# Down projections of a two-layer decoder trunk: second halves whose groups are added to the stream by DMAs, and a different set of 7-product k-tiles

## The chip, the cores and the metric

The kernel runs on one core of one Trainium2 chip. The metric is the device time of one execution in microseconds (us); lower is better. Three runs of the kernel before gave a median of 2252.42 us (2252.37 to 2252.44).

A core has TensorE (PE: matmuls, and PEld for its weight loads), VectorE (DVE), ScalarE (ACT), GpSimd (POOL) and SyncE (SP, which issues DMAs here). PE writes to PSUM banks, the other engines read and write SBUF and PSUM, and DMAs bring weights from HBM into SBUF.

## What is computed

The reference is a decoder trunk of two layers on a stream `h` of 256 tokens by 2048 features, in float32. The change lies in `conv_ffn`'s last product, `w_down`, of both layers.

```python
D_MODEL, SEQ, DEPTH, D_FF = 2048, 256, 2, 5632

def conv_ffn(xn, w_up, conv_w, conv_b, w_down):
    u = xn @ w_up
    # causal depthwise convolution of width 3 over the tokens -> c
    gate, val = jnp.split(c, 2, axis=-1)
    return (jax.nn.silu(gate) * val) @ w_down

def reference(x, ...):
    h = x
    for layer in range(DEPTH):
        if layer == 0:
            h = h + mlstm_mixer(rms_norm(h, a_norm[0]), ...)
        else:
            k_sh, v_sh = shared_kv(h, kv_norm, w_kv, positions)
            h = h + diff_attention(rms_norm(h, b_norm[0]), k_sh, v_sh, ...)
        h = h + conv_ffn(rms_norm(h, f_norm[layer]), w_up[layer], conv_w[layer],
                         conv_b[layer], w_down[layer])
    return rms_norm(h, final_norm)
```

## The kernel before

**Numbers and operands.** Every float32 operand is kept as a pair of float32r values, high and low part, and a product is made of three matmuls: high by high, low by high, high by low. The stream stays in SBUF as `stream`, 128 partitions by 2 token halves by 2048 features. Hidden features come in tiles of 128, called k-tiles.

**Weights.** They are read from HBM while the kernel runs. `granule` (from L360 on) loads 4 k-tiles by 512 columns (1 MB) into a tile `raw`, from a ring of 4 (RAW) that SP's queue fills; ACT casts the high part into a tile `w2` (L376) and DVE subtracts to make the low part (L377). `w2` has a ring of 5 tiles (HL): a cast waits until PE has used the tile that stood five before. One such pair of instructions prepares 2 k-tiles by 512 columns, or, in `gemm`, 4 k-tiles by 256.

**The down projection.** The 44 k-tiles of a layer are taken in two parts of 22, since the hidden tiles of one part fill the buffers; each part runs its up-projections (`gemm`) and then `gemm_sevenths` over four groups (NG) of 512 columns (G), and adds its result to the stream. A group accumulates both token halves in two PSUM banks (`acc`, called a and b in the code). At the k-tiles named in MIXED, four k-tiles (two at the end) are done by pairs with 7 products in place of 8, in the manner of Strassen: for two k-tiles and two token halves, 21 matmuls of width 256 stand for 12 of width 512. `sevenths` prepares their weights: DVE makes differences of weight blocks (L449 to L451), then for each pair ACT and DVE split the three plain blocks (768 elements a partition) and the four differences (1024), at L458 and L459. The sums of hidden tiles that they are multiplied with are made in the up-projection by `mix`. Parts of the products gather in two more banks (`mix`, called c and d).

**The end of a group.** `mixed_in` adds what lies in c and d to the stream: one copy by ACT (L572) and on DVE three adds of 256 (L573 to L575 and L576, with L573 and L574 making sums in the tile `mixed`) and two of 512 (L578, L579). `residual`'s `evac` then adds a and b (L587, 512 each). In layer 0's second part the attention's norm object takes the group over (`Norm.add`): ACT squares it (L224), PE transposes it a granule later (L231), and ACT and DVE make from the transposes the scaled pairs `x_at` (L306, L307) and a copy `kept` (L235). The last group of layer 1 is done apart (`finish`), the others by `evac_last`, which squares and multiplies with the last norm's gains.

**What sets the order.** The program is traced once. `tick` counts granules, and `later(n, fn)` traces a piece n granules on. The Tile scheduler then fixes each engine's instruction order by its own estimates and by what depends on what; an engine works its list strictly in this order, and semaphores hold it where an operand, a ring's tile or a bank isn't ready.

## Time and profile before

| | us |
|---|---|
| median of 3 runs | 2252.42 |
| the profiled execution | 2251.92 |
| its span, first to last instruction | 2250.0 |
| PE busy | 2238.2 |
| DVE busy | 1796.9 |
| ACT busy | 1297.7 |
| layer 0, second part: groups 0, 1, 2, 3 begin at | 1007.6, 1036.8, 1066.9, 1097.1 |
| attention's first product begins at | 1127.2 |

The times come from one profiled execution on the core. A row of groups gives the source line, engine, operation, output and inputs with their shapes, the count, and then busy time with the mean of one in ns, and the idle time just before with what released the engine. A row of the timeline gives start, length and the same names. The windows view gives the busy time of each engine in a stretch. The chain of waits is followed back from the last instruction to what released each step.

### The profile page before, as it was taken

Reading aid. Unit: us, or ns where it says so; the run is one execution under the profiler, and the core shown is the slowest. Engines: PE = TensorE matmul, PEld = TensorE weight load, DVE = VectorE, ACT = ScalarE, POOL = GpSimd, SP = SyncE. Lnnn points to the kernel's source line nnn. Section 1 sums busy time; section 2 is a strip of 40 time slices with the busy share of each in tenths; the row PEclk is TensorE's granted clock in tenths of the full one; section 3 lists DMA queues with packets and bytes.
Section 4 is the critical chain, followed back from the end, with each engine's and each line's share of the span. In section 5 each row is a group of like instructions: output and inputs, shape, how many; then the busy total and the mean of one; then the engine's idle time right before and its main releaser. Section 6 shows DMA issues by size and latency. Waiting matters only on the chain.

```text
span 2250.0 us, 33498 instructions
## 1 busy us (share of the span) xinstructions
PE 2238.2 (99%) x12859; PEld 1955.0 (87%) x12859; DVE 1796.9 (80%) x2980; ACT 1297.7 (58%) x2010; POOL 124.4 (6%) x305
## 2 busy tenths in 40 slices
...
GB/s 265 188 169 157 165 173 204 191 190 187 187 172 177 246 188 187 187 150 197 189 214 189 168 169 168 150 206 188 187 187 187 156 191 238 191 188 191 147 215 150
DMA packets 325348, 419.04 MB, mean 186 GB/s; under 512 B 9070, under 2 KB 238788, under 8 KB 325188
## 3 DMA queue, kind: packets, MB, share of 16 engines
...
q14 instruction: 59, 0.48, 0.1%
...
## 4 chain that ended last, share of the span: by engine, by line
PE 97%; DVE 1%; POOL 1%; issue 1%; ACT 0%; DMA 0%; DVEq 0%; SPq 0%; POOLq 0%
PE acc L411 54%; PE acc L503 16%; PE acc L437 12%; PE mix L493 6%; PE acc L493 4%; PE acc L634 2%; PE acc L521 1%; PE val_ps L335 1%; PE turn_ps L231 1%; POOL rs_u L279 0%; DVE w L377 0%; PE as_ps L972 0%; DMA pos_i<-in_positions_dram 0%; POOL rs_u L281 0%; PE gps L681 0%
## 5 line engine op out<-in xcount | busy, mean ns | idle before, releaser
L377 DVE TENSOR_TENSOR w<-raw,w 128x1024 fp32r<-128x1024 f32 x679 | 826.4, 1221 | 267.5 <-ACT w L376 265.6
L376 ACT ACTIVATE w<-raw 128x1024 fp32r<-128x1024 f32 x679 | 714.2, 1058 | 489.1 <-PE acc L411 322.4
L411 PE MATMUL acc<-x_f,w 128*128 128x512 f32 (+1 forms) x5632 | 987.8, 338 | 0.0
L411 PEld LDWEIGHTS acc<-x_f,w 128*128 128x128 f32 x5632 | 862.3, 188 | 122.3
L503 PE MATMUL acc<-w,hid 128*128 128x512 f32 x1080 | 268.2, 395 | 0.0
L503 PEld LDWEIGHTS acc<-w,hid 128*128 128x128 f32 x1080 | 195.5, 188 | 38.8
L411 PE MATMUL acc<-x_at,w 128*128 128x512 f32 (+1 forms) x1024 | 182.3, 338 | 0.0
L411 PEld LDWEIGHTS acc<-x_at,w 128*128 128x128 f32 x1024 | 156.8, 188 | 21.8 <-issue 0.3
L458 ACT ACTIVATE w<-diff 128x1024 fp32r<-128x1024 f32 x89 | 94.1, 1057 | 111.1 <-DVE diff L451 82.0
L417 ACT ACTIVATE low<-acc 128x256 f32<-128x256 f32 x216 | 78.8, 384 | 131.7 <-PE acc L411 128.8
L459 DVE TENSOR_TENSOR w<-diff,w 128x1024 fp32r<-128x1024 f32 x89 | 108.8, 1222 | 40.6 <-ACT w L458 39.9
L437 PE MATMUL acc<-w,x_a 128*128 128x512 f32 x576 | 138.1, 396 | 0.0
L437 PEld LDWEIGHTS acc<-w,x_a 128*128 128x128 f32 x576 | 107.0, 188 | 24.1
L493 PE MATMUL mix<-w,mix 128*128 128x256 f32 x801 | 119.5, 282 | 0.0
L418 DVE TENSOR_TENSOR acc<-acc,low 128x256 f32<-128x256 f32 x216 | 84.4, 430 | 38.6 <-ACT low L417 38.4
L493 PEld LDWEIGHTS mix<-w,mix 128*128 128x128 f32 x801 | 107.2, 188 | 2.4 <-DVE w L459 0.2
L848 ACT ACTIVATE c<-u,conv 128x256 f32<-128x256 f32 x176 | 98.2, 593 | 5.2 <-DVE u L846 4.8
L953 POOL TENSOR_TENSOR sw<-sw,sin_t 32x256 f32<-32x256 f32 x32 | 39.1, 1237 | 1043.2 <-DVE sw L952 992.7
L458 ACT ACTIVATE w<-raw 128x768 fp32r<-128x768 f32 x89 | 74.7, 839 | 37.5 <-PE acc L503 26.9
L437 PE MATMUL acc<-w,x_at 128*128 128x512 f32 x384 | 91.4, 396 | 0.0
L459 DVE TENSOR_TENSOR w<-raw,w 128x768 fp32r<-128x768 f32 x89 | 84.8, 952 | 3.0 <-ACT w L458 2.9
L493 PE MATMUL acc<-w,hid 128*128 128x256 f32 x450 | 86.4, 281 | 0.0
...
## 6 DMA issues: line engine op xcount, KB each, us to landing
...
```

The costliest lines, as they stand in the source:

```text
L376: act.activation(w2[:, :hc, 0], part, AF.Copy)
L377: dve.tensor_tensor(w2[:, :hc, 1], part, w2[:, :hc, 0].bitcast(F32), op=ALU.subtract)
L411: pe.matmul(to, a, b, start=(k == 0 and o == 0), stop=(k == kn - 1 and o == len(ops) - 1))
L417: act.activation(low, p[:, T:], AF.Copy)
L418: dve.tensor_tensor(p[:, :T], p[:, :T], low, op=ALU.add)
L437: pe.matmul(ps[t], a[:, s], b, start=(k == 0 and o == 0), stop=(k == kn - 1 and o == 2))
L458: act.activation(w2[:, :m, 0], src, AF.Copy)
L459: dve.tensor_tensor(w2[:, :m, 1], src, w2[:, :m, 0].bitcast(F32), op=ALU.subtract)
L493: pe.matmul(to, u, v, start=start and o == 0, stop=end and o == 2 and to is not a and to is not b, skip_group_check=True)
L503: pe.matmul(ps, u[:, s], v, start=(k0 + i == 0 and o == 0), stop=(k0 + i == kn - 1 and o == 2), skip_group_check=True)
L634: pe.matmul(ps[j], a, b, start=(k == 0 and o == 0 and j % 2 == 0), stop=(k == KD - 1 and o == 2), skip_group_check=True)
L848: act.activation(c, u, AF.Identity, bias=cw[:, 3, f:f + 1], scale=cw[:, 2, f:f + 1])
```

## The change

MIXED becomes two lists, one for each part. In the second part the 7-product k-tiles are now 2 to 5, 10 to 13 and 18 to 21: 12 where there were 10 (4 to 7, 12 to 15, 20 and 21). The plain k-tiles between them are 0 and 1, 6 to 9 and 14 to 17, and `granule` gets a slice of the weights for each of these stretches, so the first load of a group is half a load.

Groups 0 to 2 of layer 0's second part and groups 0 and 1 of layer 1's go through a new function `landed`. It copies part of c, and a and b, into SBUF tiles (ACT), makes the sums x and y of the mixed banks (four adds of 256 on DVE), and POOL issues four accumulating DMAs of 128 by 512 that add a, b, x and y to the stream in SBUF. What follows on the group (`Norm.add`, or `summed`, which holds the squares and gain products of `evac_last`) is traced nine granules later, and `behind` ties its squares on ACT and transposes on PE behind the last instruction traced so far on these engines. One more pair list per layer goes through `mix`. Group 3 of layer 0 and group 2 of layer 1 end as before.

```diff
@@ -38,7 +38,7 @@
 NG = D // G
 RAW = 4
 OUT_AT = (8, 10)
-MIXED = (4, 12, 20)
+MIXED = ((4, 12, 20), (2, 10, 18))
 HL = 5
 WARM, WARM_X = 28, 24
 X_AT = (0, 2, 3, 5, 6, 8, 9)
@@ -107,6 +107,17 @@
                 if i.name not in before and i.engine in last:
                     tc.add_manual_dep(i, last[i.engine], mybir.DependencyInfo(mybir.DependencyClass.NoSync, mybir.DependencyReason.DATA), reason="as_written")
                 last[i.engine] = i.name
+
+    @contextmanager
+    def behind():
+
+        traced = nc.cur_bb.bb.instructions
+        last = {i.engine: i.name for i in traced if i.engine in (act.engine, pe.engine)}
+        before = {i.name for i in traced}
+        yield
+        for i in traced:
+            if i.name not in before and i.engine in last:
+                tc.add_manual_dep(i, last[i.engine], mybir.DependencyInfo(mybir.DependencyClass.NoSync, mybir.DependencyReason.DATA), reason="behind")
 
 
     waiting, clock, loads = [], [0, 0], []
@@ -242,11 +253,17 @@
         def second(self, i):
             self.scaled(1, i, self.kept.pop(i))
 
-        def add(self, g):
-
-            self.squares(g)
+        def add(self, g, order=nullcontext):
+
+            with order():
+                self.squares(g)
+
+            def operands(i):
+                with order():
+                    self.operands(4 * g + 2 * i)
+
             for i in range(2):
-                later(1, lambda i=i: self.operands(4 * g + 2 * i))
+                later(1, lambda i=i: operands(i))
 
         def rstd(self, after=1):
 
@@ -495,7 +512,9 @@
                             tick()
                     k0 += 4
                 else:
-                    for i, (wh, wl) in enumerate(granule(w, col0 + g * G, G, k0, kn, raws, g)):
+                    since = max([0] + [k + 4 for k in at if k < k0])
+                    until = min([kn] + [k for k in at if k > k0])
+                    for i, (wh, wl) in enumerate(granule(w[since * P:until * P], col0 + g * G, G, k0 - since, until - since, raws, g)):
                         xh, xl, _ = xs[k0 + i]
                         for t, ps in enumerate((a, b)):
                             s = slice(t * P, (t + 1) * P)
@@ -578,8 +597,28 @@
         dve.tensor_tensor(both, both, u[1].rearrange("p (o n) -> p o n", o=1).broadcast_to([P, 2, T]), op=ALU.add)
         dve.tensor_tensor(stream[:, :, c0], d[:, :T].rearrange("p (o n) -> p o n", o=1).broadcast_to([P, 2, T]), stream[:, :, c0], op=ALU.add)
 
-    def residual(norm):
+    def landed(g, ps, mix, then):
+
+        (a, b), (c, d) = ps, mix
+        u = tmp("mx")
+        a2, b2, x, y = (block(F32, f"land_{n}") for n in "abxy")
+        act.activation(x[1], c[:, :T], AF.Copy)
+        dve.tensor_tensor(u, c[:, T:], x[1], op=ALU.add)
+        act.activation(a2[2], a, AF.Copy)
+        dve.tensor_tensor(y[1], d[:, T:], u, op=ALU.add)
+        act.activation(b2[2], b, AF.Copy)
+        dve.tensor_tensor(x[0], d[:, :T], u, op=ALU.add)
+        dve.tensor_tensor(y[0], d[:, :T], y[1], op=ALU.add)
+        for t, rows in ((0, a2), (1, b2), (0, x), (1, y)):
+            pool.dma_start(stream[:, t, g * G:(g + 1) * G], rows[2], accum_op=ALU.add)
+        later(9, then)
+
+    def residual(norm, by_dma=0):
+
         def evac(g, ps, mix=None):
+            if g < by_dma:
+                landed(g, ps, mix, lambda: norm.add(g, behind))
+                return
             if mix is not None:
                 mixed_in(g, mix)
             for t in range(2):
@@ -866,7 +905,7 @@
                     dve.tensor_tensor(c, c, conv_of[f], op=ALU.mult)
                     hidden[f] = split(c, f"hid{f}")
                     pair.append(c)
-                if 4 * (j // 2) in MIXED:
+                if any(k <= 2 * j < k + 4 for k in MIXED[part]):
                     mixed[2 * j] = mix(pair)
 
             for j in range(half // 2):
@@ -874,11 +913,11 @@
                 gemm(norm.sets[0], w_up[layer], D_FF + part * half * P, [j], evac_val)
             rows = w_down[layer, part * half * P:(part + 1) * half * P]
             if part == 0:
-                gemm_sevenths(hidden, mixed, rows, 0, range(NG), residual(None), MIXED)
+                gemm_sevenths(hidden, mixed, rows, 0, range(NG), residual(None), MIXED[part])
             elif finish is None:
-                gemm_sevenths(hidden, mixed, rows, 0, range(NG), evac_down, MIXED)
+                gemm_sevenths(hidden, mixed, rows, 0, range(NG), evac_down, MIXED[part])
             else:
-                gemm_sevenths(hidden, mixed, rows, 0, range(NG - 1), evac_down, MIXED)
+                gemm_sevenths(hidden, mixed, rows, 0, range(NG - 1), evac_down, MIXED[part])
                 finish(hidden, rows)
 
 
@@ -1058,7 +1097,7 @@
     gemm_sevenths(outs, outs_mixed, m_w_out[0], 0, [NG - 1], residual(norm_f0), OUT_AT[:1])
 
     norm_at = Norm([(gains, G_B), (gains, G_KV)], "at")
-    conv_ffn(0, norm_f0, residual(norm_at))
+    conv_ffn(0, norm_f0, residual(norm_at, 3))
     outs, outs_mixed = attention(norm_at)
     norm_f1 = Norm([(gains, G_F1)], "f1")
     gemm_tokens(outs, w_o[0], 0, range(2), residual(norm_f1), lead=2)
@@ -1074,24 +1113,32 @@
         return gain_rows[c0 // G][2][:, c0 % G:c0 % G + width]
 
     def evac_last(g, ps, mix=None):
-        if mix is not None:
-            mixed_in(g, mix)
         if g == 0:
 
             tc.keep_in_program_order(act.activation(work.tile([P, 1], F32, name="ahead", bufs=2), ones[:, 0:1], AF.Sqrt))
             for c in range(NG):
                 gain_rows.append(block(F32, f"gain_rows{c}"))
                 nc.sync.dma_start(gain_rows[c][2], final_norm[c * G:(c + 1) * G].rearrange("(o c) -> o c", o=1).broadcast_to([P, G]))
-        c0, width = g * G, G
-        if g == NG - 1:
-            width = T
+        if g < 2:
+            landed(g, ps, mix, lambda: summed(g, G, behind))
+            return
+        if mix is not None:
+            mixed_in(g, mix)
+        width = G if g < NG - 1 else T
         for t in range(2):
-            rows = stream[:, t, c0:c0 + width]
+            rows = stream[:, t, g * G:g * G + width]
             dve.tensor_tensor(rows, ps[t], rows, op=ALU.add)
-            act.activation(tmp("sq").bitcast(BF16)[:, :width], rows, AF.Square, accum_out=norm_out.parts[:, t, g:g + 1])
-            later(2, lambda rows=rows: dve.tensor_tensor(rows, rows, gain_cols(c0, width), op=ALU.mult))
+        summed(g, width)
         if g == NG - 1:
             later(1, sums_but_last)
+
+    def summed(g, width, order=nullcontext):
+
+        for t in range(2):
+            rows = stream[:, t, g * G:g * G + width]
+            with order():
+                act.activation(tmp("sq").bitcast(BF16)[:, :width], rows, AF.Square, accum_out=norm_out.parts[:, t, g:g + 1])
+            later(2, lambda rows=rows: dve.tensor_tensor(rows, rows, gain_cols(g * G, width), op=ALU.mult))
 
     def sums_but_last():
         for t in range(2):
```

The lines of the changed kernel stand some numbers on: the split of `granule` is L393 (ACT) and L394 (DVE), that of `sevenths` L475 and L476 with the differences at L466 to L468, `gemm`'s matmuls L428, the squares L235, the transposes L242, the scaled splits L323 and L324, `mixed_in` L591 to L598, the residual add L626, `landed` L605 to L613.

**DVE at the start of attention.** The rows of the kernel before, from the third split of attention's first product on (`w2` are weight tiles; `mixed`, `stream` and `acc` are the ending of layer 0's last group):

```order
L377 TENSOR_TENSOR w2_10960<-raw_10958,w2_10960 128x4x256
L377 TENSOR_TENSOR w2_10990<-raw_10958,w2_10990 128x4x256
L573 TENSOR_TENSOR mixed_10859<-mix_10640,mixed_10859 128x256
L575 TENSOR_TENSOR stream_149<-mix_10640,stream_149 128x256
L377 TENSOR_TENSOR w2_11038<-raw_11036,w2_11038 128x4x256
L574 TENSOR_TENSOR mixed_10859<-mix_10641,mixed_10859 128x256
L576 TENSOR_TENSOR stream_149<-stream_149,mixed_10859 128x256
L578 TENSOR_TENSOR stream_149<-stream_149,mixed_10859 128x512
L377 TENSOR_TENSOR w2_11057<-raw_11036,w2_11057 128x4x256
L579 TENSOR_TENSOR stream_149<-mix_10641,stream_149 128x2x256
L587 TENSOR_TENSOR stream_149<-acc_10580,stream_149 128x512
L587 TENSOR_TENSOR stream_149<-acc_10581,stream_149 128x512
```

The last residual add (L587) has six splits of this product ahead of it, and the sixth stands among the `mixed_in` adds. The rows of the changed kernel, from just after the sixth split on (its tiles come in the order `w2_10952`, `10997`, `11035`, `11065`, `11113`, `11132`, `11153`, `11172`; `x_at` are scaled pairs from the transposes of group 2):

```order
L324 SCALAR_TENSOR_TENSOR x_at_10_10905<-turn_ps_10900,gains_147,x_at_10_10905 128x256
L394 TENSOR_TENSOR w2_11153<-raw_11151,w2_11153 128x4x256
L324 SCALAR_TENSOR_TENSOR x_at_11_10908<-turn_ps_10900,gains_147,x_at_11_10908 128x256
L592 TENSOR_TENSOR mixed_10934<-mix_10658,mixed_10934 128x256
L594 TENSOR_TENSOR stream_149<-mix_10658,stream_149 128x256
L593 TENSOR_TENSOR mixed_10934<-mix_10659,mixed_10934 128x256
L595 TENSOR_TENSOR stream_149<-stream_149,mixed_10934 128x256
L394 TENSOR_TENSOR w2_11172<-raw_11151,w2_11172 128x4x256
L597 TENSOR_TENSOR stream_149<-stream_149,mixed_10934 128x512
L598 TENSOR_TENSOR stream_149<-mix_10659,stream_149 128x2x256
L626 TENSOR_TENSOR stream_149<-acc_10639,stream_149 128x512
L626 TENSOR_TENSOR stream_149<-acc_10640,stream_149 128x512
```

Now eight splits stand ahead of the residual adds (L626): those of `w2_11153` and `w2_11172` have moved ahead of them, with the scaled splits of group 2, and the eighth stands directly ahead of the last four adds.

**PE at the same place.** PE's rows of the kernel before around the first transposes of the last group's columns (L231):

```order
L411 MATMUL acc_10873<-x_at_11_10620,w2_10960 128x512
L411 MATMUL acc_10873<-x_at_11_10620,w2_10960 128x256
L411 MATMUL acc_10874<-x_at_11_10620,w2_10960 128x512
L411 MATMUL acc_10874<-x_at_11_10620,w2_10960 128x256
L231 MATMUL turn_ps_10896<-ident_109,stream_149 128x128
L231 MATMUL turn_ps_10909<-ident_109,stream_149 128x128
L411 MATMUL acc_11034<-x_at_0_10018,w2_11038 128x512
L411 MATMUL acc_11034<-x_at_0_10018,w2_11038 128x256
L411 MATMUL acc_11034<-x_at_1_10021,w2_11038 128x512
```

The third weight tile is read to its end, then come the transposes. The same place in the changed kernel (transposes at L242):

```order
L428 MATMUL acc_10948<-x_at_11_10908,w2_11035 128x512
L428 MATMUL acc_10948<-x_at_11_10908,w2_11035 128x256
L428 MATMUL acc_10949<-x_at_11_10908,w2_11035 128x512
L428 MATMUL acc_10949<-x_at_11_10908,w2_11035 128x256
L242 MATMUL turn_ps_10971<-ident_109,stream_149 128x128
L242 MATMUL turn_ps_10984<-ident_109,stream_149 128x128
L428 MATMUL acc_11109<-x_at_0_10270,w2_11113 128x512
L428 MATMUL acc_11109<-x_at_0_10270,w2_11113 128x256
```

The transposes stand where they stood, behind the last matmul with the third weight tile (`w2_10960` before, `w2_11035` now); the matmuls ahead of them now read `x_at_11` from a split that DVE makes four instructions before the adds begin.

**ACT at the end of layer 0's group 1.** ACT's rows of the kernel before, from the split of the next group's first plain blocks on (L224 are the squares of group 1):

```order
L458 ACTIVATE w2_10355<-raw_10349 128x3x256
L572 ACTIVATE mixed_10273<-mix_10054 128x256
L458 ACTIVATE w2_10358<-diff_10351 128x4x256
L458 ACTIVATE w2_10361<-raw_10349 128x3x256
L458 ACTIVATE w2_10364<-diff_10351 128x4x256
L376 ACTIVATE w2_10411<-raw_10409 128x2x512
L224 ACTIVATE sq_10283,parts_at_3914<-stream_149 128x512
L224 ACTIVATE sq_10285,parts_at_3914<-stream_149 128x512
L376 ACTIVATE w2_10426<-raw_10409 128x2x512
L458 ACTIVATE w2_10447<-raw_10441 128x3x256
```

The squares come four casts behind the one copy. The same place in the changed kernel, where group 1 lands (`land_x`, `land_a`, `land_b`) and its squares are L235:

```order
L246 ACTIVATE kept2_10289<-turn_ps_10278 128x512
L605 ACTIVATE land_x_10315<-mix_10036 128x256
L607 ACTIVATE land_a_10313<-acc_10017 128x512
L475 ACTIVATE w2_10450<-diff_10443 128x4x256
L609 ACTIVATE land_b_10314<-acc_10018 128x512
L475 ACTIVATE w2_10453<-raw_10441 128x3x256
L475 ACTIVATE w2_10456<-diff_10443 128x4x256
L393 ACTIVATE w2_10503<-raw_10501 128x2x512
L393 ACTIVATE w2_10518<-raw_10501 128x2x512
L475 ACTIVATE w2_10543<-raw_10537 128x3x256
L235 ACTIVATE sq_10533,parts_at_3914<-stream_149 128x512
L235 ACTIVATE sq_10535,parts_at_3914<-stream_149 128x512
```

One copy of 256 has become one of 256 and two of 512, which stand among the casts of `sevenths`; the squares have moved to five casts behind the last copy.

2 lines of the change are left out of this document (1 added, 1 removed).

## The prediction

> **What bounds the kernel now.** I read the busy times first, then the chain of work that ended last, then the windows view cut at the starts of the column groups that change.
>
> ```profile
> PE 2238.2 (99%) x12859; PEld 1955.0 (87%) x12859; DVE 1796.9 (80%) x2980; ACT 1297.7 (58%) x2010; POOL 124.4 (6%) x305
> PE 97%; DVE 1%; POOL 1%; issue 1%; ACT 0%; DMA 0%; DVEq 0%; SPq 0%; POOLq 0%
> ```
>
> TensorE (PE) is busy 99% of the span and makes 97% of the chain. So a matmul less is time won, and time in which PE stands still is lost in full; nothing else counts. The windows show what stands behind PE in the stage of the change (columns: stretch, its length, then busy time and number of instructions of PE, PEld, DVE, ACT, POOL, granted clock, DMA share, GB/s):
>
> ```profile
> 900.00:1000.00 100.00, 100.00 (x573) 87.42 (x572) 80.53 (x137) 58.28 (x90) 0.00 (x0) 1.00 0.55 177
> 1007.60:1036.80 29.20, 29.20 (x179) 25.95 (x178) 27.19 (x41) 17.34 (x23) 0.00 (x0) 1.00 0.52 174
> 1036.80:1066.90 30.10, 30.10 (x187) 26.83 (x186) 28.19 (x38) 19.56 (x28) 0.00 (x0) 1.00 0.54 182
> 1066.90:1097.10 30.20, 30.20 (x188) 26.95 (x187) 28.51 (x38) 19.48 (x28) 0.00 (x0) 1.00 0.56 191
> 2180.30:2209.60 29.30, 29.28 (x178) 25.91 (x178) 26.85 (x35) 15.66 (x20) 0.00 (x0) 1.00 0.59 191
> ```
>
> The first row is an up-projection: PE full, VectorE (DVE) 81%, room on all engines. The next three are groups 0, 1 and 2 of layer 0's second down projection, the last is group 2 of layer 1's. PE never stops there either, but DVE is busy 28.2 us of 30.1. PE and DVE run at nearly one rate, so a delay put on DVE, or on ScalarE (ACT) ahead of it, isn't regained inside a group. How little room there is shows in the timeline where group 2 begins (columns: start, length, engine, line, operation, count, idle time before and its releaser):
>
> ```profile
> 1067.88 1.06 ACT L458 ACTIVATE w<-diff 128x1024 fp32r<-128x1024 f32 x1 [0.70 <-DVE diff L451]
> 1069.63 1.22 DVE L459 TENSOR_TENSOR w<-diff,w 128x1024 fp32r<-128x1024 f32 x1
> 1072.23 1.22 DVE L459 TENSOR_TENSOR w<-diff,w 128x1024 fp32r<-128x1024 f32 x1
> 1073.23 1.11 PE L493 MATMUL acc<-w,hid 128*128 128x256 f32 x8
> 1074.18 0.52 PE L493 MATMUL acc<-w,mix 128*128 128x256 f32 x3
> ```
>
> The second split of differences ends at 1072.23+1.22 = 1073.45. PE comes to the products that use it in its rows of 1073.23 and 1074.18: the split is at most 0.7 us ahead of its need.
>
> **The change part by part.** *Two more k-tiles in 7 products.* For 2 k-tiles and both token halves, 12 matmuls of width 512 become 21 of width 256. The chain of waits has a clean run of each:
>
> ```profile
> 368.44 16.75 PE acc L503 x72
> 2211.09 15.01 PE acc L437 x128
> ```
>
> One 512 costs 16.75/72 = 0.2326 us, one 256 costs 15.01/128 = 0.1173. A pair saves 12 x 0.2326 - 21 x 0.1173 = 0.33 us. Seven groups change (four in layer 0, three in layer 1; the last of layer 1 is another function): **-2.3 us**. All of it is on PE, so all of it counts, if PE gets its operands.
>
> *What the engines do for it.* The durations:
>
> ```profile
> L376 ACT ACTIVATE w<-raw 128x1024 fp32r<-128x1024 f32 x679 | 714.2, 1058 | 489.1 <-PE acc L411 322.4
> L377 DVE TENSOR_TENSOR w<-raw,w 128x1024 fp32r<-128x1024 f32 x679 | 826.4, 1221 | 267.5 <-ACT w L376 265.6
> L459 DVE TENSOR_TENSOR w<-raw,w 128x768 fp32r<-128x768 f32 x89 | 84.8, 952 | 3.0 <-ACT w L458 2.9
> L451 DVE TENSOR_TENSOR diff<-raw,diff 128x512 f32<-128x512 f32 x2 | 1.4, 685 | 0.0
> L573 DVE TENSOR_TENSOR mixed<-mix,mixed 128x256 f32<-128x256 f32 x1 | 0.4, 417 | 0.0
> L235 ACT ACTIVATE kept<-turn_ps 128x512 f32<-128x512 f32 x2 | 1.2, 578 | 0.0
> L572 ACT ACTIVATE mixed<-mix 128x256 f32<-128x256 f32 x2 | 0.8, 385 | 2.2 <-PE mix L493 2.2
> L417 ACT ACTIVATE low<-acc 128x256 f32<-128x256 f32 x216 | 78.8, 384 | 131.7 <-PE acc L411 128.8
> L418 DVE TENSOR_TENSOR acc<-acc,low 128x256 f32<-128x256 f32 x216 | 84.4, 430 | 38.6 <-ACT low L417 38.4
> ```
>
> On DVE a plain pair's split (1.22) becomes two splits (0.95+1.22) and its share of differences (half of 1.22 + 0.69 + 0.69, so 1.30): +2.25. Landing takes off evacuation: three adds of 256 and four of 512 (3 x 0.42 + 4 x 0.69 = 4.0) become four of 256 (1.7), so -2.3. DVE is left where it was, at PE's rate, with no lead won. ACT gets +1.0 for one more split (0.84+1.06 against 1.06) and two copies of 512 (0.58 each). The other mix per layer falls in the up-projections, whose window leaves DVE 19% and ACT 42% idle: I cost it at 0; without that cover it would be its few short adds, a 512 cast and a 512 subtract, under 3 us once per layer. The load slices differ, their sum (5.5 MB) and number (6) per group don't: 0.
>
> *The group heads.* In the five landed groups the next group's head on ACT now has three copies (0.39 + 0.58 + 0.58) where one of 0.39 stood, +1.2 us, queued ahead of the casts of the differences; behind each cast wait its DVE split and PE. The lead that was there is at most 0.7. Each head so costs between 1.2 - 0.7 = 0.5 and 1.2: over five, 2.5 to 6.0. In groups 2 and 3 of layer 0 and 2 of layer 1 it falls together with the squares and transposes of the group before, which now come nine granules later, into the next head; there I go to the upper end, in the two others to the lower: 2 x 0.5 + 3 x 1.1 = **+4.3 us**.
>
> *The start of attention.* This is the largest term. The last group of layer 0 isn't landed; it still goes through `mixed_in` and the adds, and PE's first transposes of the last columns wait for them. Before, it went like this:
>
> ```profile
> 1127.18 8.59 PE L411 MATMUL acc<-x_at,w 128*128 128x512 f32 x48
> 1130.25 1.06 ACT L376 ACTIVATE w<-raw 128x1024 fp32r<-128x1024 f32 x1 [1.47 <-PE acc L411]
> 1131.50 1.22 DVE L377 TENSOR_TENSOR w<-raw,w 128x1024 fp32r<-128x1024 f32 x1
> 1132.63 0.69 DVE L579 TENSOR_TENSOR stream<-mix,stream 128x512 f32<-128x512 f32 x1
> 1133.36 1.29 DVE L587 TENSOR_TENSOR stream<-acc,stream 128x512 f32<-128x512 f32 x2
> 1135.61 0.38 PE L231 MATMUL turn_ps<-ident,stream 128*128 128x128 f32 x2
> ```
>
> The adds ended at 1134.65, and PE, busy with the first product of attention, came to the transposes at 1135.6 without a stop. The order of the changed kernel puts more splits ahead of the adds: the last one, `w2_11172`, is the fifth tile after `w2_11035` in a ring of five (HL), so its cast can only start when PE has read `w2_11035` for the last time, and on PE that is the instruction directly ahead of the transposes. PE then stands until a cast (1130.25 to 1131.50, 1.25 with the hand-over), the split (1.13 to the next start), two `mixed_in` adds and the first residual add (3 x 0.69) have run, and two hand-overs of some 0.1: **4.6 us**. Shortly before, `x_at_11`, queued behind the split of `w2_11153`, has the same wait on the slot of `w2_10997`: a cast, a split and a 0.48 scaled split, 2.9 us, against three k-tiles of PE work (12 matmuls at 8.59/48 = 0.18, so 2.15): +0.8. Behind the stop, DVE is late by a queue of splits, and the first bank handed back through L417 and L418 comes late by up to those two: +0.8. **+6.2 us**, bounds 4.6 (both small ones covered) and 7.2.
>
> *The landing itself.* Before's trace has no accumulating transfer and none issued by POOL. The nearest row is a load of 1 MB:
>
> ```profile
> 1088.26 0.37 SPq L446 DMA_DIRECT2D raw<-in_w_down_dram  x1
> 1093.45 1.22 DVE L449 TENSOR_TENSOR diff<-raw 128x1024 f32<-128x1024 f32 x1 [0.91 <-DMA raw<-in_w_down_dram]
> ```
>
> It took 5.2 us from issue to use. A landing moves 256 KB, and two go in series (x waits for a, y for b). The squares behind them stand on ACT with weight casts queued after; from the copy of b to the square there lie five casts in groups 2 and 3, and five DVE splits of 1.1 to 1.2 with the differences between make about 8 us. Up to 4 us each the pair hides: 0. At 5.2 each it is late by 2.4 in up to three such places: at most +7. A quarter of the bytes should take less than 5.2, so I take 0 and keep 7 for the range; at 8 us each the pair would be 8 late in three places: +24.
>
> The Trainium skill, "DMA: Bandwidth & Descriptors", section "Anatomy of one DMA — SWDGE (gpsimd) path", gives a GpSimd DMA about 2.0 us and its bytes over 436 GB/s; an estimate by it is 2.6 us for 256 KB, 5.2 for the pair, and the sum would stay as it is.
>
> **Sum**: -2.3 + 4.3 + 6.2 + 0 = +8.2 us. The profiled execution took 2251.92, so 2260.1; the median of the runs is 0.5 above it, so **2260.6 us**. Its own range: heads 2.5 to 6.0, attention 4.6 to 7.2, landing 0 to 3: 2257.2 to 2266.3.
>
> **Rivals.** *My reading of the ring is wrong (not slower).* The place is the cast of `w2_11172`. If its slot was free at an earlier read, DVE works through the row without a stop, the adds end about 1134.65 as before, ahead of PE's 1135.6, and a DVE that has lost no time covers the heads too. The gain stands: 2252.4 - 2.3 = 2250.1, within 0.2%. It decides at 1 us of lead before the transposes. For it: PE was never stopped there. Against: the ring has five tiles, and just four (`w2_11065`, `11113`, `11132`, `11153`) are made between the two.
>
> *The heads are covered, attention isn't.*
>
> ```profile
> 1030.77 1.22 DVE L377 TENSOR_TENSOR w<-raw,w 128x1024 fp32r<-128x1024 f32 x1
> 1036.81 0.40 PE L503 MATMUL acc<-w,hid 128*128 128x512 f32 x1
> ```
>
> The plain split for group 1's first matmul ends at 1031.99, 4.8 us before PE reads it. If such a lead lasts through the head, the heads cost 0: 2252.4 - 2.3 + 6.2 = 2256.3. It decides at 1.2 us of lead on the differences' splits. Against: those had 0.7 at most at the head of group 2.
>
> *Landing is slow.* POOL issues four transfers in a row while weight loads take 52 to 59% of the DMA engines (windows above), and a square that waits holds ACT's casts. By the bounds above: 2260.6 + 3 to + 24, so 2264 to 2285. For it: no row shows the operation. Against: one quarter of the bytes of a 5.2 us load.
> The Trainium skill speaks for this rival in "SBUF — State Buffer", section "SBUF: two separate sides": a DMA that POOL issues can be held back while DVE runs an operation that takes both of its ports, since POOL can't write its descriptors. No run here shows it; DVE's work in these windows is subtraction of two tensors.
>
> **How the numbers follow.** Forecast 2260.6: 0.64. Slow landing: 0.15. Heads covered: 0.12. Ring misread: 0.09. The range leaves out the last and the far end of the slow landing: 2253 to 2272. About 0.2% (4.5 us) is what a measurement here can tell from no change. Faster than 2247.9: 0.02, only if both savings count and more; within 0.2%: 0.09 + 0.12 and a tail of the forecast, less that 0.02, so 0.22; slower: 0.76.
>
> **What would show it.** In the changed kernel's windows, seven groups shorter by 0.33 us of PE work, with PE's busy time below the stretch in the landed groups. A stop of 4 to 5 us on PE ahead of the first transposes (L242) at attention's start, released by the residual add (L626), and a split (L394) whose ACT cast waited for PE just before it. At the heads, casts (L475) behind copies L605, L607, L609. The squares (L235) should not wait for a DMA; if they do, for several us, landing is slow. Wrong it is if PE goes on through L242 without a stop, or if the heads show none.

## The result and the profile after

The changed kernel takes 2273.4 us (median of 5 runs, 2270.57 to 2274.07); the kernel before took 2252.38 in the same comparison (2252.13 to 2252.44). The ratio is 1.0092, 95% interval 1.0081 to 1.0103: slower by 21.0 us. The forecast was 2260.6 with a range of 2253 to 2272: the direction was right, the time lies outside the range. The runs of the kernel before lie within 0.3 us of each other, those of the changed kernel within 3.5.

The profiled execution took 2270.57, its span is 2268.8. The page's rows of busy time and of the chain that ended last:

```profile
PE 2245.1 (99%) x12922; PEld 1958.6 (86%) x12922; DVE 1801.3 (79%) x2977; ACT 1305.3 (58%) x2029; POOL 142.4 (6%) x325
PE 92%; DVE 3%; DMA 2%; issue 1%; ACT 1%; POOL 1%; DVEq 0%; SPq 0%; ACTq 0%; POOLq 0%
```

PE's share of the chain has gone from 97% to 92%; DVE, ACT and, new, DMAs are in it now. The windows of the changed kernel (columns as before: stretch, length, busy time and count of PE, PEld, DVE, ACT, POOL, granted clock, DMA share, GB/s) for the four groups of layer 0's second part, and the last group of layer 1's that goes through `gemm_sevenths`:

```profile
1007.30:1037.40 30.10, 30.10 (x195) 27.20 (x194) 27.44 (x40) 17.26 (x22) 0.00 (x0) 1.00 0.53 172
1037.40:1067.80 30.40, 30.37 (x194) 27.17 (x194) 26.67 (x31) 18.51 (x26) 3.67 (x4) 1.00 0.71 203
1067.80:1098.70 30.90, 30.23 (x193) 26.65 (x192) 26.81 (x33) 20.30 (x30) 3.43 (x4) 1.00 0.71 205
1098.70:1133.00 34.30, 32.06 (x197) 27.63 (x196) 28.08 (x35) 22.60 (x32) 3.47 (x4) 1.00 0.78 226
2197.00:2229.60 32.60, 30.21 (x188) 26.20 (x188) 27.27 (x33) 19.46 (x26) 3.46 (x4) 1.00 0.80 230
```

The last four rows are the groups in which the group before lands. DVE has 27 to 28 us of work there and PE is no longer full; the DMA share is 0.71 to 0.80, against 0.52 to 0.59 in the prediction's windows of the kernel before and 0.53 in the first row, where nothing lands yet. The difference is the landing's traffic.

**Where the time went.** PE's program is nearly the same in both kernels, so the start of one and the same kind of instruction can be set against its start in the kernel before. I took five places from the two traces: A, the first product of layer 0's second down projection (1007.59 before); B, the last matmul into the mixed banks of its group 3 (1126.71); C, the 301st matmul of attention's products with `x_at` (1181.27); D, the first product of layer 1's second down projection (2122.83); E, the last matmul into the mixed banks of its group 2 (2210.69). The lag is the start in the kernel named less the start before, in the profiled executions:

| kernel | A | B | C | D | E | end of span |
|---|---|---|---|---|---|---|
| the changed kernel | -0.3 | 6.0 | 13.7 | 14.1 | 18.6 | 18.8 |
| 12 k-tiles only (e1) | -0.3 | 6.2 | 10.7 | 10.9 | 16.8 | 17.1 |
| landing only (e2) | 0.3 | 8.7 | 15.3 | 17.0 | 16.7 | 17.0 |
| half landing (e3) | 0.2 | 2.0 | 9.8 | 10.8 | 11.8 | 11.9 |
| adds first (e4) | 0.6 | 8.8 | 13.4 | 14.0 | 20.7 | 20.9 |
| same traffic (e5) | 0.3 | 3.8 | 11.5 | 12.2 | 15.7 | 16.0 |
| no sums (e6) | -0.4 | 1.1 | 9.5 | 9.4 | 10.3 | 10.4 |
| POOL adds (e7) | 0.3 | 10.2 | 18.9 | 19.2 | 26.8 | 26.9 |
| first groups (e8) | 1.1 | 3.1 | 6.3 | 7.9 | 11.0 | 11.1 |
| 12 k-tiles, adds first (e9) | 0.3 | 8.1 | 7.9 | 7.7 | 13.8 | 13.9 |
| layer 1 only (e10) | 0.5 | 0.5 | 0.5 | 0.5 | 4.9 | 5.1 |
| layer 1, landing only (e11) | 0.4 | 0.4 | 0.4 | 0.4 | 0.2 | 0.4 |
| layer 1, two groups (e12) | 0.2 | 0.2 | 0.2 | 0.2 | 2.9 | 3.0 |

So the changed kernel loses 6.2 us in layer 0's four groups (6.0 + 0.3, rounded), 7.7 at the start of attention, and 4.4 in layer 1's groups; the rest of the program runs as before. The saved matmuls are in these sums already. Two cautions. The changed kernel's profiled execution is the fastest of its five, 2.8 us under the median, so its lags add up to 18.8 and not to 21.0. And the idle times in PE's rows don't add up to the lags: in layer 0's groups those over 0.15 us make 2.8 us. The rest are matmuls that start a tenth or two late one after another, mostly at the same places.

**The start of attention.** The timeline of the changed kernel there (start, length, engine, line, operation, count, idle before and its releaser):

```profile
1141.30 0.97 PE L428 MATMUL acc<-x_at,w 128*128 128x512 f32 x4 [1.00 <-DVE x_at L324]
1142.37 1.06 ACT L393 ACTIVATE w<-raw 128x1024 fp32r<-128x1024 f32 x1 [0.21 <-PE acc L428]
...
1143.53 1.22 DVE L394 TENSOR_TENSOR w<-raw,w 128x1024 fp32r<-128x1024 f32 x1
1144.66 0.68 DVE L597 TENSOR_TENSOR stream<-stream,mixed 128x512 f32<-128x512 f32 x1
1145.38 0.69 DVE L598 TENSOR_TENSOR stream<-mix,stream 128x512 f32<-128x512 f32 x1
1146.10 1.29 DVE L626 TENSOR_TENSOR stream<-acc,stream 128x512 f32<-128x512 f32 x2
...
1146.94 0.66 PE L242 MATMUL turn_ps<-ident,stream 128*128 128x128 f32 x2 [4.67 <-DVE stream L626]
...
1164.77 7.48 PE L428 MATMUL acc<-x_at,w 128*128 128x512 f32 x41 [0.66 <-DVE aq L989]
```

The rows stand in the order in which they release one another: PE's last read of the slot lets ACT cast `w2_11172`, DVE splits it, makes two `mixed_in` adds and the first residual add, and 4.67 us after its last matmul PE goes on. `x_at_11` had come 1.00 late before that, and a bank comes 0.66 late behind it. These three make 6.3 of the 7.7 us. The rest is put down to the clock, in the windows during and behind the stop (the column after POOL's is the granted clock):

```profile
1140.00:1145.00 5.00, 1.27 (x6) 0.61 (x4) 4.06 (x8) 1.93 (x3) 0.00 (x0) 0.88 1.09 348
1145.00:1150.00 5.00, 3.06 (x11) 2.71 (x12) 3.78 (x13) 1.34 (x4) 0.00 (x0) 0.50 0.92 285
1150.00:1155.00 5.00, 5.00 (x32) 4.45 (x32) 2.17 (x10) 0.96 (x3) 0.00 (x0) 0.94 0.01 3
```

PE works again from 1146.94, but at half the clock: 3.1 us of work in this window are worth 1.5 at full speed, and 0.06 of the next window's 5 us are another 0.3. These 1.8 us (an estimate) are near the 1.4 left over.

**The landing.** The profile's list of DMA issues (queue, count, size, median us from issue to landing) has, for the five landed groups:

```profile
stream<-land_a POOLq DMA_DIRECT2D x5, 256.0 KB, 4.1
stream<-land_b POOLq DMA_DIRECT2D x5, 256.0 KB, 5.4
stream<-land_x POOLq DMA_DIRECT2D x5, 256.0 KB, 6.2
stream<-land_y POOLq DMA_DIRECT2D x5, 256.0 KB, 6.7
```

By these medians a pair in series takes 4.1 + 6.2 = 10.3 to 5.4 + 6.7 = 12.1 us. How this comes to PE is seen in layer 0's group 3, where group 2 lands; there the pair of a and x takes 13.7 us (1110.25 to 1123.98):

```profile
1110.25 0.86 POOL L613 DMA_DIRECT2D stream<-land_a  x1 [22.99 <-ACT land_a L607]
1110.79 1.21 POOL L613 DMA_DIRECT2D stream<-land_b  x1
...
1117.44 0.86 POOL L613 DMA_DIRECT2D stream<-land_x  x1 [5.44 <-DMA stream<-land_b]
1118.79 0.86 POOL L613 DMA_DIRECT2D stream<-land_y  x1 [0.48 <-issue]
...
1123.98 0.63 ACT L235 ACTIVATE sq<-stream 128x512 bf16<-128x512 f32 x1 [6.05 <-DMA stream<-land_x]
...
1125.52 0.63 ACT L235 ACTIVATE sq<-stream 128x512 bf16<-128x512 f32 x1 [0.81 <-DMA stream<-land_y]
1126.15 1.04 ACT L475 ACTIVATE w<-diff 128x1024 fp32r<-128x1024 f32 x1
...
1127.24 0.73 PE L510 MATMUL mix<-w,mix 128*128 128x256 f32 x4 [1.28 <-ACT w L475]
```

The row of land_x names land_b as what released it. By the tiles it is land_a that x waits for; land_a took 6.7 us and was down by 1116.9, land_b took 7.5, to 1118.3, which is after x was issued.

ACT stands 6.05 us at the first square and 0.81 at the second; the cast behind them (L475) comes late, and PE waits for it. All four waits of squares for landings lie in layer 0 (11.6 us in all). And the traffic holds up weight loads: the waits view gives for DVE's first difference of a load (us in total, times, longest)

```profile
DVE diff L466 <- DMA raw<-in_w_down_dram: 5.0, 6, 2.4
```

That is the whole program. In layer 1's groups it is 3.2 us, where the kernel before has none; in layer 0's groups it is 0.5, less than the 1.8 of the kernel before (L449). The longest, in layer 1's group 2, reaches PE: the load comes 9.0 us after its issue, where the prediction's row had 5.2.

```profile
2207.73 0.37 SPq L463 DMA_DIRECT2D raw<-in_w_down_dram  x1
...
2216.72 1.22 DVE L466 TENSOR_TENSOR diff<-raw 128x1024 f32<-128x1024 f32 x1 [2.38 <-DMA raw<-in_w_down_dram]
...
2219.13 3.06 PE L522 MATMUL acc<-w,hid 128*128 128x512 f32 x12 [1.00 <-DVE w L394]
```

### The profile page after: what moved, and what is told of

Same layout as the page of the kernel before. It is cut to its first block, busy times and chain, and to the rows that moved or that the text cites. A ratio compares the mean times of both kernels' runs of the same rounds, so it can differ in the third digit from the quotient of the medians.

```text
span 2268.8 us, 33695 instructions
## 1 busy us (share of the span) xinstructions
PE 2245.1 (99%) x12922; PEld 1958.6 (86%) x12922; DVE 1801.3 (79%) x2977; ACT 1305.3 (58%) x2029; POOL 142.4 (6%) x325
## 4 chain that ended last, share of the span: by engine, by line
PE 92%; DVE 3%; DMA 2%; issue 1%; ACT 1%; POOL 1%; DVEq 0%; SPq 0%; ACTq 0%; POOLq 0%
PE acc L428 53%; PE acc L522 13%; PE acc L454 12%; PE mix L510 5%; PE acc L510 3%; PE acc L673 2%; DMA raw<-in_w_down_dram 1%; DVE w L394 1%; DVE w L476 1%; PE acc L540 1%; PE val_ps L352 1%; PE turn_ps L242 1%; DVE diff L466 0%; POOL rs_u L296 0%; ACT w L475 0%
## 5 line engine op out<-in xcount | busy, mean ns | idle before, releaser
L394 DVE TENSOR_TENSOR w<-raw,w 128x1024 fp32r<-128x1024 f32 x672 | 816.6, 1220 | 259.4 <-ACT w L393 257.4
L428 PE MATMUL acc<-x_f,w 128*128 128x512 f32 (+1 forms) x5632 | 987.8, 337 | 0.0
L393 ACT ACTIVATE w<-raw 128x1024 fp32r<-128x1024 f32 x672 | 705.7, 1057 | 459.8 <-PE acc L428 317.5
L428 PEld LDWEIGHTS acc<-x_f,w 128*128 128x128 f32 x5632 | 862.2, 188 | 122.4
L522 PE MATMUL acc<-w,hid 128*128 128x512 f32 x996 | 250.4, 395 | 2.0 <-DVE w L394 2.0
L522 PEld LDWEIGHTS acc<-w,hid 128*128 128x128 f32 x996 | 179.4, 188 | 38.1 <-DVE w L394 2.9
L428 PE MATMUL acc<-x_at,w 128*128 128x512 f32 (+1 forms) x1024 | 184.1, 340 | 1.7 <-DVE x_at L324 1.0
L428 PEld LDWEIGHTS acc<-x_at,w 128*128 128x128 f32 x1024 | 157.9, 190 | 24.1 <-DVE x_at L324 1.3
L475 ACT ACTIVATE w<-diff 128x1024 fp32r<-128x1024 f32 x96 | 101.4, 1056 | 128.1 <-DVE diff L468 100.8
L476 DVE TENSOR_TENSOR w<-diff,w 128x1024 fp32r<-128x1024 f32 x96 | 117.2, 1221 | 53.7 <-ACT w L475 53.4
L510 PE MATMUL mix<-w,mix 128*128 128x256 f32 x864 | 134.4, 283 | 2.4 <-ACT w L475 2.2
L510 PEld LDWEIGHTS mix<-w,mix 128*128 128x128 f32 x864 | 117.5, 188 | 8.0 <-ACT w L475 3.2
L613 POOL DMA_DIRECT2D stream<-land_a x5 | 4.5, 905 | 1569.1 <-ACT land_a L607 1569.1
L475 ACT ACTIVATE w<-raw 128x768 fp32r<-128x768 f32 x96 | 80.5, 839 | 34.1 <-PE acc L522 19.3
L510 PE MATMUL acc<-w,hid 128*128 128x256 f32 x492 | 98.4, 281 | 0.0
L476 DVE TENSOR_TENSOR w<-raw,w 128x768 fp32r<-128x768 f32 x96 | 91.3, 951 | 3.3 <-ACT w L475 2.8
```

Source lines behind the costliest of these rows:

```text
L393: act.activation(w2[:, :hc, 0], part, AF.Copy)
L394: dve.tensor_tensor(w2[:, :hc, 1], part, w2[:, :hc, 0].bitcast(F32), op=ALU.subtract)
L428: pe.matmul(to, a, b, start=(k == 0 and o == 0), stop=(k == kn - 1 and o == len(ops) - 1))
L475: act.activation(w2[:, :m, 0], src, AF.Copy)
L476: dve.tensor_tensor(w2[:, :m, 1], src, w2[:, :m, 0].bitcast(F32), op=ALU.subtract)
L510: pe.matmul(to, u, v, start=start and o == 0, stop=end and o == 2 and to is not a and to is not b, skip_group_check=True)
```

## The experiments

Two theories and the landing stood against each other. Theory 1 is the prediction's: a group's head pays for ACT's three copies. Theory 2: it is DVE, which the 12 k-tiles overfill and the landing only relieves again. Theory 3: the accumulating DMAs themselves. All ratios are to the kernel before on the same chip, with 95% intervals.

**e1, the 12 k-tiles alone.**

```diff
-    conv_ffn(0, norm_f0, residual(norm_at, 3))
+    conv_ffn(0, norm_f0, residual(norm_at))
...
-        if g < 2:
+        if g < 0:
             landed(g, ps, mix, lambda: summed(g, G, behind))
```

> The 12 k-tiles in 7 products stay; no group lands, all end through mixed_in and the residual adds as before. Theory 1 (on record: a group's head pays for ACT's landing copies): no copies, no stops at the heads; -2.3 us of matmuls, and the stop at attention's start with one split and one residual add after PE's last read of the slot (1.25 + 1.13 + 0.7 + 0.1 = 3.2), with the slow clock and the late bank behind it as in the changed kernel (1.9 + 0.8): 2252.4 - 2.3 + 5.9 = 2256. Theory 2 (DVE is overfilled by the 12 k-tiles: 2.25 us more per group, which landing only gives back): DVE needs 28.2 + 2.25 = 30.4 us and some 2 of waits for ACT per group against 29.8 on PE, 2.6 x 7 = 18 less the 8 us of lead at a stage's start: 2266, between 2262 and 2270, with stops on PE in the middle of groups. Theory 3 (the accumulating DMAs cost the time): as theory 1, 2256.

Measured 2270.52, ratio 1.0083 (1.0068 to 1.0098): the 12 k-tiles alone cost 18 us, nearly as much as the whole change, without a copy or a DMA of the landing. Theory 2's time is this one, half a us above its span; theory 1 and 3 miss by 14. The window of layer 1's group 2 and two rows of PE in its group 1:

```profile
2194.20:2226.70 32.50, 30.41 (x189) 26.63 (x188) 30.02 (x38) 17.84 (x23) 0.00 (x0) 1.00 0.61 198
```

```profile
2173.07 4.89 PE L522 MATMUL acc<-w,hid 128*128 128x512 f32 x20 [0.48 <-DVE w L394]
2179.91 0.74 PE L510 MATMUL mix<-w,mix 128*128 128x256 f32 x4 [1.13 <-ACT w L475]
```

DVE is busy 30.0 us, 3.2 more than in this group before (26.85), and the group is 3.2 longer (32.5 against 29.3): it grows by what DVE's work grows, as theory 2 has it. In layer 1 PE also waits in the middle of groups.

But this edit changes two things: there are more 7-product k-tiles, and the first of them stand two k-tiles sooner in the group (at 2 in place of 4). Where layer 0's group 1 begins, DVE isn't behind with its work. It stands idle for ACT's copy, which waits for PE's last product into the mixed banks; the adds, the last difference and a cast follow, and PE is there first:

```profile
1037.29 0.39 ACT L591 ACTIVATE mixed<-mix 128x256 f32<-128x256 f32 x1 [3.81 <-PE mix L510]
1037.71 0.42 DVE L592 TENSOR_TENSOR mixed<-mix,mixed 128x256 f32<-128x256 f32 x1 [1.83 <-ACT mixed L591]
...
1040.27 0.50 PE L510 MATMUL acc<-w,hid 128*128 128x256 f32 x2 [0.45 <-ACT w L475]
```

And the cast behind PE's stop at 2179.91 had waited 6.14 us for PE to free a weight tile, 0.1 us longer than for DVE's difference. So the earlier place and the ring of five tiles are rivals of theory 2; no run changes the place alone.

**e2, the landing alone.**

```diff
-MIXED = ((4, 12, 20), (2, 10, 18))
+MIXED = ((4, 12, 20), (4, 12, 20))
```

> The landing stays, the 7-product k-tiles are those of before (10 in each part). Theory 1 (ACT's copies at the heads): heads cost 4.3 as on record, attention's start 6.2 to 8.5: 2263 to 2265. Theory 2 (DVE overfilled): DVE has 2.3 us less to do per landed group than before, so no stops at the heads; what is left is the stop at attention's start, where the order has a split ahead of the last three adds (1.25 + 1.13 + 3 x 0.7 + 0.1 = 4.6, slow clock 1.9, late bank 0.8): 2259 to 2260. Theory 3 (DMAs): as theory 2 and the wait of the squares for the second pair, 2 to 5 us: 2262 to 2265, and runs that differ by some us.

Measured 2268.64, ratio 1.0074 (1.0057 to 1.0091). Each theory's number is too low. The lags say why: layer 1's groups cost nothing (17.0 to 16.7), copies and DMAs and all, and layer 0's cost 8.4. There the squares feed the transposes of the next norm, and ACT waited for landings again; the waits view, and PE's row after the wait of 5.2 (the one of 6.3 is followed by a stop of 1.56):

```profile
ACT sq L235 <- DMA stream<-land_x: 9.2, 2, 6.3
ACT sq L235 <- DMA stream<-land_y: 5.2, 1, 5.2
```

```profile
1129.04 0.80 PE L510 MATMUL mix<-w,hid 128*128 128x256 f32 x2 [3.94 <-ACT w L475]
```

So theory 3's mechanism is there, larger than it was put. Theory 1 has nothing left in layer 1: the same three copies stand there and no head stops.

**e3, half the landing.** Only a and b are added by DMA; what the mixed banks hold doesn't reach the stream.

```diff
-        for t, rows in ((0, a2), (1, b2), (0, x), (1, y)):
+        for t, rows in ((0, a2), (1, b2)):
```

> The changed kernel with only the DMAs of a and b; those of x and y are left out, so the stream lacks what the mixed banks hold and the output isn't the reference's. ACT's copies and DVE's four adds stay. A square waits for one DMA instead of two in series. Theory 3 (the serial pair is late, and how late differs between runs): 2268 to 2271, no square (L235) waits for a DMA, and the runs lie within 1 us of each other. Theories 1 and 2: the same time as the changed kernel, 2271 to 2274.

Measured 2263.97 (2263.61 to 2265.75), ratio 1.0053 (1.0038 to 1.0068): 9.4 us less than the changed kernel, more than theory 3 asked for, and the runs are closer together. The waits of squares for DMAs go from 11.6 us to 1.0, those of L466 for loads from 5.0 to 1.6, the latter all outside the groups of the change. The lag goes from 6.2 to 1.7 in layer 0's groups and from 4.4 to 1.0 in layer 1's; at attention it stays (7.8).

**e4, the changed kernel with the adds first.** From the sixth on, casts and splits of attention's first product are tied behind the last group's copy (ACT) and last residual add (DVE).

```diff
...
         act.activation(w2[:, :hc, 0], part, AF.Copy)
+        after_last(6, 1)
         dve.tensor_tensor(w2[:, :hc, 1], part, w2[:, :hc, 0].bitcast(F32), op=ALU.subtract)
+        after_last(6, 2)
...
```

> The changed kernel with an order laid on the start of attention: from the sixth on, the casts and splits of its first product stay behind the copy and the residual adds of layer 0's last group on ACT and DVE. Theory (on record): the stop ahead of the transposes comes from the split that stands before the adds; it shrinks from 4.7 to about 2 (the adds now end after the scaled splits of group 2 only), x_at_11 and the first bank come in time, and the slow clock after the stop goes in part: 2273.4 - 4.5 to 2273.4 - 7, 2266.5 to 2269. Rival (PE would stop there anyway, for the transposes' other operands): within 1.5 us of 2273.4.

Measured 2269.29 (2266.09 to 2272.67), ratio 1.0075 (1.006 to 1.009): 4.1 less, just short of the expected span, while the runs spread over 6.6 us. The stop ahead of the transposes shrank from 4.67 only to 3.53, since the adds still came behind group 2's scaled splits; `x_at_11` and the bank no longer stop PE. In the profiled runs the lag at attention goes from 7.7 to 4.6. The theory holds in its direction, with a smaller effect; the runs of the two kernels overlap, and e9 tests it without the landing.

**e5, the same traffic without the wait.** The DMAs of x and y land in the tiles of a and b.

```diff
-        for t, rows in ((0, a2), (1, b2), (0, x), (1, y)):
+        for t, rows in ((0, a2), (1, b2)):
             pool.dma_start(stream[:, t, g * G:(g + 1) * G], rows[2], accum_op=ALU.add)
+        for to, rows in ((a2, x), (b2, y)):
+            pool.dma_start(to[2], rows[2], accum_op=ALU.add)
```

> The changed kernel with the DMAs of x and y landing in the SBUF tiles land_a and land_b (each still behind the DMA of a or b) in place of the stream: same bytes, same order, but no square waits for the second pair. The stream lacks what the mixed banks hold, the output isn't the reference's. The half landing took 2264.0, the changed kernel 2273.4. If the 9.4 us between them are the squares' wait for the serial pair: about 2264, no wait of L235 for land_x or land_y. If they are what the traffic does to the weight loads (DVE and ACT waiting for raw tiles): about 2273. Half and half: 2268 to 2269.

Measured 2268.13, ratio 1.0075 (1.0059 to 1.009): half and half. Of the 9.4 us, 4.1 (2268.1 - 2264.0) come with the traffic alone: ACT and DVE have the same order of instructions in e3 and e5, their runs don't overlap, and the ends of their profiled runs differ by 4.1 too. The other 5.3 (2273.4 - 2268.1) are put down to the squares' wait for the second pair. This part is less sure: the profiled runs differ by 2.8, the runs touch, and at two places ACT's cast stands elsewhere in the order. In the profiled run of e5 DVE's differences wait for loads as in the changed kernel, 5.4 us in all.

**e6, half the landing and no sums.** DVE's four adds in `landed` are left out too; ACT's copies stay.

```diff
...
         act.activation(x[1], c[:, :T], AF.Copy)
-        dve.tensor_tensor(u, c[:, T:], x[1], op=ALU.add)
         act.activation(a2[2], a, AF.Copy)
-        dve.tensor_tensor(y[1], d[:, T:], u, op=ALU.add)
...
```

> The half landing (DMAs of a and b only) without DVE's four adds of 256 in landed; ACT's three copies stay where they are. What the mixed banks hold is lost, the output isn't the reference's. It takes 4 x 0.34 to 0.42 = 1.4 to 1.7 us from DVE per landed group. Theory 2 (the stops at the heads come from DVE being at PE's rate): the 5.0 us of stops that the half landing still has in the five groups behind landed ones (2.7 in the lags and the 2.3 that the products save) go nearly all: 2264.0 - 3 to - 5, 2259 to 2261. Theory 1 (they come from ACT's copies ahead of the casts): 2263 to 2264.

Measured 2261.18, ratio 1.004 (1.0026 to 1.0054): 2.8 less than e3, just above theory 2's span. In the profiled run the stops at heads and in the middle of layer 0's groups 2 and 3 were gone, but one of 1.58 came at a square that waited for the DMA of b, 7.0 us after its issue (1078.75 to 1085.72):

```profile
1078.75 1.21 POOL L608 DMA_DIRECT2D stream<-land_b  x1
...
1085.72 0.63 ACT L235 ACTIVATE sq<-stream 128x512 bf16<-128x512 f32 x1 [1.76 <-DMA stream<-land_b]
...
1087.23 0.51 PE L510 MATMUL mix<-w,hid 128*128 128x256 f32 x2 [1.58 <-ACT w L475]
```

It speaks against theory 1, since ACT's copies are still there. It doesn't measure theory 2 cleanly: fewer adds on DVE also shorten the chain at the heads.

**e7, POOL adds in place of the DMAs.** All of the work is done.

```diff
-            pool.dma_start(stream[:, t, g * G:(g + 1) * G], rows[2], accum_op=ALU.add)
+            at = stream[:, t, g * G:(g + 1) * G]
+            pool.tensor_tensor(at, rows[2], at, op=ALU.add)
```

> The changed kernel with the four accumulating DMAs replaced by four adds of 512 on POOL (all of the work is done). From the one row that before has (32x256 in 1.24 us) an add of 512 takes about 2.5 us, the two that follow each other 5 in place of the 10 to 13 of the DMA pair. If the DMAs' lateness and traffic are worth 9.4: 2264 to 2266. Rival (POOL's adds slow DVE's subtractions while they run, 4 x 2.5 us in each of five groups): a subtract of 1024 takes longer than 1.22 us, and the time stays above 2268.

Measured 2278.2, ratio 1.0115 (1.0101 to 1.0128): the slowest of all. The adds are shorter than expected (1.7 to 2.1 us each in the mean), but DVE's subtractions run longer while they last; two group rows of this kernel (mean ns of one before the second bar's idle time), and one subtraction beside an add:

```profile
L476 DVE TENSOR_TENSOR w<-diff,w 128x1024 fp32r<-128x1024 f32 x96 | 126.0, 1313 | 48.0 <-ACT w L475 47.6
L476 DVE TENSOR_TENSOR w<-raw,w 128x768 fp32r<-128x768 f32 x96 | 97.0, 1011 | 3.2 <-ACT w L475 2.6
1040.71 2.30 DVE L476 TENSOR_TENSOR w<-diff,w 128x1024 fp32r<-128x1024 f32 x1 [0.19 <-ACT w L475]
1041.90 2.27 POOL L614 TENSOR_TENSOR stream<-land_x,stream 128x512 f32<-128x512 f32 x1
```

The mean over all 96 went from 1221 to 1313 and from 951 to 1011, though POOL adds only in five groups: the eight of 1024 that overlap an add took 2.30 us in the mean, the others 1.22. That is the rival's outcome.

**e8, 12 k-tiles in the first groups only**, on the kernel before, without landing.

```diff
+            at = first if first and g == 0 else rest
...
-                gemm_sevenths(hidden, mixed, rows, 0, range(NG), residual(None), MIXED)
+                gemm_sevenths(hidden, mixed, rows, 0, range(NG), residual(None), MIXED, (4, 12, 18))
```

> The kernel before, with 12 k-tiles in 7 products (4 to 7, 12 to 15, 18 to 21) in group 0 of each of the four down projections and nowhere else; no landing. All of the work is done. DVE comes to a first group with 7 to 9 us of lead, and 12 k-tiles cost it 2.25 us: theory 2 says the lead pays for that, but the groups behind run at PE's rate and meet a lead of 2.25 less, with stops of up to 1 us each at three heads: between 2252.3 - 4 x 0.33 = 2251.0 and 2254. If the groups behind are not touched: 2251.0.

Measured 2262.93, ratio 1.0051 (1.0038 to 1.0064), a miss by 9 us. Layer 0's groups lose 2.0, attention 3.3, layer 1's groups 3.1. At attention PE stops for 3.1 us at the transposes again, in a kernel without any landing and with a group 3 that is unchanged: the scheduler's order there turned over with a change three groups earlier. Again one split (L377) stands directly ahead of the residual adds and waits for ACT's cast, and the cast for PE. The stop is that order's, not the landing's.

**e9, e1 with the adds first** (the edit of e4 on e1).

> The 12 k-tiles alone (first experiment, 2270.5) with the order of the fourth at attention's start: from the sixth on, casts and splits of the first product stay behind the last group's copy and residual adds. There the order had one split directly ahead of the residual adds; the profile has a stop of 3.1 and 4.5 us of lag between the last group's end and the middle of that product. Theory (the stop is the split's place in the order, whatever put it there): the stop goes, 2270.5 - 3 to - 4.5, 2266 to 2267.5; what is left (stops in the middle of groups, 12 us in both layers) is DVE's. Rival (the stop comes from DVE's backlog after four overfilled groups): it stays within 1 us of 2270.5.

Measured 2265.83 (2265.7 to 2265.93), ratio 1.0061 (1.0047 to 1.0074): 4.7 less than e1, a little more than expected. PE goes through the transposes without a stop, and the clock stays at 1.00 (windows of e9 there):

```profile
1140.00:1145.00 5.00, 5.00 (x32) 4.35 (x31) 4.47 (x6) 2.86 (x5) 0.00 (x0) 1.00 1.03 312
1145.00:1150.00 5.00, 5.00 (x33) 4.48 (x31) 3.34 (x10) 2.55 (x6) 0.00 (x0) 1.00 1.07 360
```

The stop of 3.1 is gone; the bank's of 0.65 stays, at 0.52. The lag at attention goes from 4.5 to -0.2, so some 1.4 us went with the stop beyond its 3.1 and the 0.13. The slow clock fits this. After e1's stop of 3.10 the clock was at 0.68 in the mean over 5 us; e8 has a stop of 3.10 at the same place and kept the full clock, and there attention lost 3.3 in place of 4.5 (first row e1, second e8):

```profile
1144.00:1149.00 5.00, 4.60 (x20) 4.03 (x21) 3.30 (x17) 1.33 (x4) 0.00 (x0) 0.68 1.04 334
1141.00:1146.00 5.00, 4.79 (x30) 4.29 (x31) 3.22 (x18) 1.81 (x5) 0.00 (x0) 1.00 0.96 311
```

**e10, the whole change in layer 1 only.**

```diff
-MIXED = ((4, 12, 20), (2, 10, 18))
+MIXED = (((4, 12, 20), (4, 12, 20)), ((4, 12, 20), (2, 10, 18)))
...
-    conv_ffn(0, norm_f0, residual(norm_at, 3))
+    conv_ffn(0, norm_f0, residual(norm_at))
...
```

> The whole change in layer 1 alone (12 k-tiles, groups 0 and 1 landed, squares 9 granules behind); layer 0 and attention's start have the order of before. From the lag of the changed kernel over layer 1's groups (14.1 to 18.6): 2252.3 + 4.4 = 2256.7, or 2255 to 2258 as the landings vary. Rival (layer 1 only pays for the state in which layer 0 leaves it): 2251.3, the gain of three groups.

Measured 2256.75 (2255.57 to 2260.2), ratio 1.0022 (1.0012 to 1.0032), as expected. Layer 1's 4.4 us are its own.

**e11, the landing alone in layer 1 alone** (e2's MIXED, e10's layer 0).

> Only the landing, only in layer 1 (groups 0 and 1); 10 k-tiles as before everywhere. Theory 2 (DVE's load decides, the copies and DMAs are hidden where DVE has room): the lag over layer 1's groups in the second experiment was -0.3, so 2252.0 to 2252.4, no stop at the heads. Theory 1 (ACT's copies cost 0.5 to 1.2 at each of two heads): 2253.3 to 2254.7.

Measured 2252.04, ratio 0.9999 (0.999 to 1.0008), no difference. At a landed head of it, ACT makes the copies and the cast behind them comes while PE still has plain matmuls to do:

```profile
2152.33 5.75 PE L522 MATMUL acc<-w,hid 128*128 128x512 f32 x24
2152.46 0.59 ACT L607 ACTIVATE land_a<-acc 128x512 f32<-128x512 f32 x1
2152.93 0.61 ACT L609 ACTIVATE land_b<-acc 128x512 f32<-128x512 f32 x1
...
2154.93 1.06 ACT L475 ACTIVATE w<-diff 128x1024 fp32r<-128x1024 f32 x1 [1.39 <-DVE diff L468]
```

The cast waited 1.39 us for DVE's difference, not for the copies. Theory 1 is refuted for these heads, which have four plain k-tiles ahead of the first 7-product set; in the changed kernel there are two. DVE waits for loads here too (1.9 us at L466 in layer 1's groups) and nothing is lost: a late load costs where DVE has no lead left.

**e12, layer 1's landing with 12 k-tiles in just the two landed groups.**

```diff
...
-                gemm_sevenths(hidden, mixed, rows, 0, range(NG - 1), evac_down, MIXED[part])
+                gemm_sevenths(hidden, mixed, rows, 0, range(NG - 1), evac_down, MIXED[part], (4, 12, 18), (0, 1))
...
```

> The landing of layer 1's groups 0 and 1, and in just these two groups 12 k-tiles in 7 products (4 to 7, 12 to 15, 18 to 21, so that only one more pair is mixed); the rest as before. All of the work is done. Theory 2: landing frees 2.3 us of DVE per landed group and two more k-tiles take 2.25, the stage's lead is untouched: 2252.3 - 2 x 0.33 = 2251.6. If the longer chain of splits stops PE at a head or a landing is late: 2253 to 2255.

Measured 2254.09, ratio 1.0006 (0.9998 to 1.0015): not faster, 1.9 us above the kernel before by the medians, with an interval that reaches to no difference. In its profiled run layer 1's groups lose 2.7. Of PE's three longest stops there, two (0.44 and 0.54) come behind a difference that waited for a load (0.94 and 1.51), and one of 0.89 behind a difference that DVE made after the two gain products. No version tried beats the kernel before.

## Why the prediction was wrong

- **What bounds the kernel**: right. All of the loss lies in the stages of the change, as stops and late starts of PE and as time at a lower clock.
- **The gain of 2.3 us**: not measured by itself, since each kernel with the 12 k-tiles had stops too; the lags contain it.
- **The start of attention (+6.2)**: right in each part, and short by one. Stop 4.67 (4.6 predicted), `x_at_11` 1.00 (0.8), bank 0.66 (0.8). What was left out is the clock during and after a stop, some 1.4 us: measured 7.7. e9 shows that the place of the split makes the stop; e8 and e1 show that it needs no landing.
- **The heads (+4.3)**: the size came out near, but by luck, since the runs don't bear out the cause given for it. e3, which has the copies and little wait for DMAs, loses 1.7 + 1.0 = 2.7 in the groups; with the 2.3 saved that is 5.0. But with four plain k-tiles ahead the copies alone cost nothing (e11, and layer 1 of e2), and the 12 k-tiles, without copies, cost 6.5 + 5.9 in the groups (e1), 14.7 with the saving. The prediction had "DVE is left where it was, at PE's rate, with no lead won", and then charged the loss to ACT's 1.2 us. It left out that the first 7-product set comes two k-tiles sooner: 12 x 0.2326 = 2.8 us less of PE's work ahead of it, against a lead that it read as 0.7. Its balance for DVE is off too: `mixed_in` has four adds of 256 (L573 to L576), not three, so a landing takes 2.7 us off DVE, not 2.3. e1 and e8 point to DVE, whose work grows by more than a group can hold (e8's later groups have the k-tiles of before and lose as well). What DVE's load and what the earlier place costs isn't separated.
- **The landing (0)**: this is the step that failed. "A quarter of the bytes should take less than 5.2, so I take 0 and keep 7 for the range" measured 4.1 to 6.7 us each, 10 to 12 a pair against a cover of 8, and cost 9.4 us (changed kernel against e3): 4.1 through the traffic (e3 and e5), which was not in the prediction, and 5.3 by the medians for squares that wait. A quarter of the bytes of the nearest row took about as long as that row's 5.2 us.
- **The sum** with measured terms: heads less saving 2.7, attention 7.8 and 1.0 between C and D from e3's profile, and 9.4 between e3 and the changed kernel make 20.9, against 21.0. It comes out by the way it is made, and shows only where the terms lie. The predicted terms (-2.3, 4.3, 6.2, 0) make 8.2; 9.4 of the 12.7 missing are the landing, 1.6 attention, 1.0 the stretch from C to D and 0.7 the heads.
- **The rivals**: slow landing, with a chance of 0.15, named the right mechanism and 2264 to 2285. The sign given for it, a square that waits several us for a DMA, is there (6.05). It put the lateness at the squares and had no term for the traffic. The ring was read rightly, and heads weren't covered. The range's upper end of 2272 cut into this rival, and the time lay just above.

What stays open: how a landing's traffic delays loads (whether in the queues, or in the engines that move the bytes); what the heads would cost with 12 k-tiles whose first set stands at 4 in every group; and why the whole change costs little more than each half of it alone (e1 18.2, e2 16.3, both 21.0).
